# The first expert's first two column blocks: for all tokens, or for gathered tokens like the rest

## The chip, the cores and the metric

The kernel runs on one core of a Trainium2 chip. The metric is the device time of one execution in microseconds (us); lower is better. All times inside the program are counted from the first instruction of the profiled execution.

## The reference

A decoder trunk of two layers on 256 tokens of width 1024 (float32). The first layer ends in a dense channel mixer; the second ends in a mixture of eight experts, and that is the part this change touches:

```python
def swiglu(x, w_gu, w_down):
    gu = jnp.einsum('bsd,df->bsf', x, w_gu)
    g, u = gu[..., :D_FF], gu[..., D_FF:]
    return jnp.einsum('bsf,fd->bsd', jax.nn.silu(g) * u, w_down)

def moe_swiglu(x, w_router, w_gu, w_down):
    logits = jnp.einsum('bsd,de->bse', x, w_router).astype(jnp.float32)
    top_logits, top_idx = lax.top_k(logits, TOP_K)
    top_gates = jax.nn.softmax(top_logits, axis=-1)
    gates = jnp.sum(jax.nn.one_hot(top_idx, N_EXPERTS, dtype=jnp.float32) * top_gates[..., None], axis=-2)
    out = jnp.zeros_like(x)
    for e in range(N_EXPERTS):
        out = out + gates[..., e:e + 1] * swiglu(x, w_gu[e], w_down[e])
    return out
```

D_FF is 2816 (22 blocks of 128 columns), TOP_K is 2 and N_EXPERTS is 8. One expert's weights are 33 units of 1024 KB: 22 for `w_gu`, 11 for `w_down`.

## The kernel before

All weights come through one `Stream` (class at L67). Its list of pieces has a fixed order, a piece is at most 1024 KB, and a piece is loaded as soon as the program knows a free slot for it; in the expert stage there are 17 such slots. The loads are issued by SyncE (SP) in program order, and each waits until TensorE is done with the piece that held the slot. `st.whole()` takes the next piece, `st.passed()` gives its slot back and issues the next load.

An expert's 22 column blocks are cut into chunks, `CH`. A step (e, c) is one chunk of one expert: `up` multiplies the gathered rows of the expert (`xg`, 64 of them) with the chunk's columns of `w_gu`, `up_more` does 32 further rows if the expert has more than 64 tokens (a branch, `more_than_half`), and then `down_both` does the rows of `w_down` that belong to the step before. A step of eight blocks has eight up pieces, which are all given back after the step's branch; only in one step, that of `groups`, are they taken in four groups of two, each with a branch of its own. Small jobs (turning the one-hot matrices, loading counts, the gates) wait in the list `tasks`, and `some(n)` does the next n of them.

Between the last layer norm and the first step stands the router (`first_step`): turn the rows (`turn_rows`), the `logits`, `select` the two best, `number` the tokens of each expert, `count` them, `choose` which expert comes last, build the one-hot matrices (`one_hots`, the first task) and gather (`gather`, eight times). Before the change, the first two column blocks of expert 0 need no gather: `first_columns` multiplies all 256 tokens with them while the router runs, `first_hidden` applies the gate function, and `first_gather` picks expert 0's tokens from the result afterwards:

```python
    def first_columns(pt, tb, k0, k1):
        for k in range(k0, k1):
            mm(pt, xf[tb][:, k], pcs[k // 4][:, k % 4], start=(k == 0))
```

The two pieces that `first_columns` takes are given back by the two calls of `st.passed()` in `first_step`. The loop at the end of `experts` then skips step (0, 0). The rest of the order is written out by hand; nothing reorders it.

Of the kernel before, what the change touches and what calls it, by code (L numbers as in the profile page):

```python
# [12 lines left out]
F32 = mybir.dt.float32  # L13
F32R = mybir.dt.float32r
BF16 = mybir.dt.bfloat16
I32 = mybir.dt.int32
AF = mybir.ActivationFunctionType
OP = mybir.AluOpType
AX = mybir.AxisListType

P = 128
D = 1024
KT = 8
S = 256
TB = 2
# [5 lines left out]
NE = 8  # L31
HALF = 64
CAP = 96
# [12 lines left out]
def trunk_kernel(ctx: ExitStack, tc: tile.TileContext, x, mem, positions, w_in_a, conv_a, w_q_b,  # L46
                 w_kv_shared, w_mem_kv, w_o, ln1_g, ln1_b, ln2_g, ln2_b, w_gu_dense, w_down_dense,
                 w_router, w_gu_moe, w_down_moe, out):
    nc = tc.nc
# [8 lines left out]
    def banks(n=2):  # L58
        return [psum.tile([P, 512], F32, name="pa", tag="pa", bufs=4) for _ in range(n)]

    def bank():
        return psum.tile([P, 512], F32, name="pb", tag="pb", bufs=4)

    def mm(o, l, r, start, stop=True):
        nc.tensor.matmul(o, l, r, start=start, stop=stop, skip_group_check=True)  # L65
# [148 lines left out]
    st = Stream()  # L214
# [3 lines left out]
    def rows(w):  # L218
        return w.rearrange("(k p) c -> p k c", p=P)

    def split(hi, lo, src):
        nc.scalar.copy(hi, src)  # L222
        nc.vector.tensor_sub(lo, src, hi)  # L223
# [21 lines left out]
    def last(gen, tasks=(), every=1):  # L245

        tasks, v = list(tasks), None
        for i, v in enumerate(gen):
            if i % every == every - 1 and tasks:
                t = tasks.pop(0)  # L250
                if t:
                    t()
        for t in tasks:
            if t:
                t()
        return v
# [201 lines left out]
    st.add(*cols(w_kv, MIX, 512), *cols(w_kv, MIX + 512, 256), *wo_specs(1))  # L458


    CH = [[(0, 2), (2, 8), (10, 8), (18, 4)]] + [[(0, 8), (8, 8), (16, 6)]] * (NE - 1)
    order = list(range(FIXED))
    STEPS = [(e, c) for e in range(NE) for c in range(len(CH[e]))]

    def expert_matrix(w, e):

        return w[0, e] if e < FIXED else w[0, bass.ds(order[e], 1)].rearrange("o a b -> (o a) b")

    def expert_up(e, c):
        f0, nf = CH[e][c]  # L470
        w, step = nf * P, PC // (2 * nf * P)

        def piece(k):
            return expert_matrix(w_gu_moe, e).rearrange("(k p) (s f) -> p k s f", p=P, s=2)[
                :, k:k + step, :, f0 * P:f0 * P + w]
        return [(lambda k=k: piece(k), (step, 2, w)) for k in range(0, KT, step)]

    def expert_down(e, c):
        f0, nf = CH[e][c]
        return [(lambda j=j: rows(expert_matrix(w_down_moe, e))[:, f0 + j:f0 + j + 2], (2, D))  # L480
                for j in range(0, nf, 2)]
# [73 lines left out]
    v = last(prod_ws(5, 4, xh, xl), [None, None, load_mem])  # L555
# [6 lines left out]
    v = last(prod_ws(2, 4, xh, xl))  # L562
# [3 lines left out]
    def conv_taps(i):  # L566
        nc.vector.tensor_scalar(yT[:, i], zT[:, i, 2:], cw[:, 12 + i:13 + i], None, op0=OP.mult)
        for k in (1, 0):
            nc.vector.scalar_tensor_tensor(yT[:, i], zT[:, i, k:k + S], cw[:, 6 * k + i:6 * k + i + 1],
                                           yT[:, i], op0=OP.mult, op1=OP.add)  # L570
# [3 lines left out]
    v = last(prod_ws(2, 4, xh, xl), turns, every=2)  # L574
# [5 lines left out]
    v = last(prod_ws(1, 2, xh, xl), [lambda: conv_taps(0), None, lambda: conv_taps(1), None, lambda: conv_taps(2)])  # L580
# [28 lines left out]
    def gate_out(v, i0):  # L609
        for h in range(len(v)):  # L610
# [4 lines left out]
    v = last(prod_ws(2, 4, xh, xl), [None, None, None, units[0].transp, None, units[1].transp, units[0].values,  # L615
                                     units[1].values])
    gate_out(v, 0)
    v = last(prod_ws(1, 2, xh, xl))
# [14 lines left out]
    pcs = []  # L633
# [21 lines left out]
    hT = {}  # L655
# [58 lines left out]
    pcs = st.get(TAIL)  # L714
# [69 lines left out]
    def turn_task(store, tb, i0, n, keys):  # L784
        return lambda: turn_heads(store[tb], tb, i0, n, keys)

    kt, qt = {}, {}
    pcs = st.get(3)
    for tb in range(TB):
        pt = banks()  # L790
# [5 lines left out]
    v = last(prod_ws(1, 2, xh, xl), [None, turn_task(kt, 0, 0, 4, True), None, turn_task(kt, 0, 4, 2, True)])  # L796
# [4 lines left out]
    pcs = st.get(3)  # L801
    pt = banks()
# [3 lines left out]
    pt = banks()  # L806
# [4 lines left out]
    pcs = st.get(3)  # L811
# [14 lines left out]
    pcs = st.get(1)  # L826
# [33 lines left out]
    xf = {}  # L860
# [20 lines left out]
    moe = ctx.enter_context(pool("moe"))  # L881
# [23 lines left out]
    def row_parts(tb):  # L905
        nc.scalar.copy(xth[:, tb], x3[:, tb])
        nc.vector.tensor_sub(xtl[:, tb], x3[:, tb], xth[:, tb])
# [16 lines left out]
        nc.vector.scalar_tensor_tensor(slot, sel, -OFF, ps[:, :2 * NE].rearrange("p (t e) -> p t e", t=TB),  # L924
                                       op0=OP.mult, op1=OP.add)

    pcs = [st.whole() for _ in range(2)]
    hd = {}

    def first_columns(pt, tb, k0, k1):  # L930

        for k in range(k0, k1):
            mm(pt, xf[tb][:, k], pcs[k // 4][:, k % 4], start=(k == 0))

    def first_hidden(tb, pt):
        h = moe.tile([P, 512], F32, name="h", tag="h", bufs=2)
        nc.scalar.activation(h[:, :256], pt[:, :256], AF.Silu)
        nc.vector.tensor_tensor(h[:, :256], h[:, :256], pt[:, 256:], op=OP.mult)
        hd[tb] = moe.tile([P, 2, 256], F32R, name="hd", tag="hx", bufs=2)
        split(hd[tb][:, 0], hd[tb][:, 1], h[:, :256])  # L940

    def router_gates():
        nc.vector.tensor_reduce(mx, lg, axis=AX.X, op=OP.max)
        nc.vector.tensor_tensor(pe, lg, mx[:, :, None].to_broadcast(T3), op=OP.subtract)
# [52 lines left out]
    def experts(part):  # L997
        xg, oneh, turned, hs, hxs, hts, htxs, ys = {}, {}, {}, {}, {}, {}, {}, {}
        tasks = []
# [38 lines left out]
        def groups(e, c):  # L1038

            n = len(expert_up(e, c))  # L1040
            return [2] * (n // 2) if part == 0 and (e, c) == STEPS[1] else [n]

        def up(e, c, n):

            w = CH[e][c][1] * 64
            if up.k == 0:
# [21 lines left out]
        def up_more(e, c, pcs, k):  # L1068
            w = CH[e][c][1] * 64
            g, px = xg[e], up_more.to  # L1070
# [11 lines left out]
        def turn(e, c):  # L1082
            n = CH[e][c][1] // 2
            h = hs.pop((e, c))
# [55 lines left out]
        def scatter_tasks(e):  # L1140
            return [lambda tb=tb, h=h: scatter(e, tb, h) for h in range(2) for tb in range(TB)]

        def first_gather():

            ps = bank()
            for i in range(2):
                for tb in range(TB):
                    for j in range(2):
                        mm(ps[:, i * CAP:(i + 1) * CAP], hd[tb][:, j, i * P:(i + 1) * P], oneh[0][:, tb],
                           start=(i == tb == j == 0))  # L1150
            hts[0, 0] = moe.tile([P, 8, HALF], F32, name="hT", tag="hT", bufs=2)
            htxs[0, 0] = moe.tile([P, 8, CAP - HALF], F32, name="hTx", tag="hTx", bufs=2)
            v = ps[:, :2 * CAP].rearrange("p (a b) -> p a b", a=2)
            nc.scalar.copy(hts[0, 0][:, :2], v[:, :, :HALF])
            nc.vector.tensor_copy(htxs[0, 0][:, :2], v[:, :, HALF:])

        def first_step(gathers):
            pt = banks(2)
            first_columns(pt[0], 0, 0, KT)
            logits(0)  # L1160
            turn_rows(1)
            row_parts(0)
            first_hidden(0, pt[0])
            logits(1)
            select()
            row_parts(1)
            first_columns(pt[1], 1, 0, 6)
            number()
            count()
            first_columns(pt[1], 1, 6, KT)  # L1170
            for _ in range(2):
                st.passed()
            gathers[0]()
            choose()
            for t in gathers[1:1 + KT]:
                t()
            load_orders()
            first_hidden(1, pt[1])
            load_count(0)

        def first_acc():
# [35 lines left out]
        t = batch_tasks(BATCHES[0])  # L1217
        prev = STEPS[0]
        if part == 0:
            first_step(t)  # L1220
            tasks += [first_gather] + t[1 + KT:] + [first_acc]
        else:
            for f in t:
                f()
        for i, (e, c) in enumerate(STEPS):
            if (e, c) == (NE - 1, 2):
                st.retire(raw3)
            for b in BATCHES[1:]:
                if e == b[0] - 1 and c == 0:
                    tasks += batch_tasks(b)  # L1230
            if part == 0 and i == 0:
                continue
            (up_more.to,) = banks(1)
            for g, n in enumerate(groups(e, c)):
                k = up.k
                pcs = up(e, c, n)
                if g == 0:
                    some(3)
                    hxs[e, c] = moe.tile([P, 512], F32, name="hx", tag="hx", bufs=2)
                if g == 0 and i > 0:  # L1240
                    turn_both(prev, prev[0] == e, lambda: up_more(e, c, pcs, k))
                else:
                    with more_than_half(e):
                        up_more(e, c, pcs, k)
                for _ in pcs:
                    st.passed()
            if i > 0:
                down_both(prev, prev[0] == e)
                if prev[1] == len(CH[prev[0]]) - 1:
                    rows_split(prev[0])  # L1250
                    tasks += scatter_tasks(prev[0])
            prev = e, c
# [48 lines left out]
```

## Time and profile before

| what | value |
|---|---|
| median of 3 runs | 1150.37 us (1148.99 to 1150.81) |
| the profiled execution, its own time | 1151.92 us |
| its span, first to last instruction | 1150.2 us |
| TensorE (PE) busy | 1079.8 us, 94% of the span |
| VectorE (DVE) busy | 374.0 us, 33% |
| ScalarE (ACT) busy | 255.4 us, 22% |
| moved by the transfers | 353.79 MB, 308 GB/s over the span |

The profiled execution lies 1.55 us above the median of the three runs. A busy TensorE includes matmuls that run slowly, so its 94% is not a measure of how close it is to its peak. The granted clock of a stretch is 1.00 at 2.4 GHz and 0.50 at 1.2 GHz.

### The profile page before, as it was taken

What the parts mean: (1) busy time and instruction counts of PE and PEld (TensorE: products, weight loads), DVE (VectorE), ACT (ScalarE), POOL (GpSimd) and SP (SyncE); (2) the same over time, 40 slices, a digit from 0 to 9 for tenths busy, and PEclk for the clock granted to TensorE, in tenths of its full rate; (3) what the DMA queues carried; (4) which work ended last, traced back from release to release, by engine and by line L of the source; (5) the groups of instructions that cost most, each with busy time, mean ns of one, the idle gap of its engine ahead of it and who ended that gap; (6) DMA issues with size and microseconds to landing.
All of it is one profiled execution on the core that took longest, in us unless ns stands there. A gap on an engine that the chain in (4) does not pass through costs nothing. (4 is left out here: it accounts for less than half of the span.)

```text
span 1150.2 us, 17136 instructions
## 1 busy us (share of the span) xinstructions
PE 1079.8 (94%) x6958; PEld 640.7 (56%) x6958; DVE 374.0 (33%) x616; ACT 255.4 (22%) x379; POOL 31.7 (3%) x46
## 2 busy tenths in 40 slices
PE   8999999999999899999979998999998999999992
PEld 7988999999887676343323443343333343333330
DVE  5678655454766647010001101100200101200205
ACT  5453544443246522010000000100100100100100
POOL 1000000000100000000000000000000000000002
PEclk9999999999999999998999999899999999999996
DMA  9646565556353369889999999899999999999991
GB/s 332 218 152 215 181 222 199 184 168 216 114 183 126 130 230 361 319 335 408 404 408 409 404 408 409 324 378 402 392 405 409 406 406 409 401 372 404 405 405 51
DMA packets 127590, 353.79 MB, mean 308 GB/s; under 512 B 6375, under 2 KB 41968, under 8 KB 127488
## 3 DMA queue, kind: packets, MB, share of 16 engines
q1 hardware_dynamic: 127392, 352.35, 80.5%
q8 instruction: 69, 1.13, 0.4%
q14 instruction: 33, 0.27, 0.1%
q0 software_dynamic: 96, 0.04, 0.0%
HBM read 351.32 MB, written 1.05 MB: 306 GB/s over the span
## 5 line engine op out<-in xcount | busy, mean ns | idle before, releaser
L65 PE MATMUL pa<-raw,xg 128*64 128x512 f32 (+4 forms) x2304 | 384.6, 555 | 9.3 <-DMA raw<-in_w_gu_moe_dram 8.9
L65 PEld LDWEIGHTS pa<-raw,xg 128*64 128x64 f32 (+1 forms) x2304 | 136.1, 128 | 245.6 <-issue 216.2
L65 PE MATMUL pb<-raw,hT 128*64 128x512 f32 x704 | 161.7, 611 | 6.9 <-ACTq L1196 2.9
L139 DVE TENSOR_TENSOR lo<-raw,hi 128x2048 fp32r<-128x2048 f32 (+2 forms) x68 | 148.5, 2194 | 48.9 <-ACT hi L129 48.8
L65 PE MATMUL pa<-xh,hi 128*128 128x256 f32 x528 | 150.7, 285 | 0.2 <-ACT xh L222 0.2
L129 ACT CAST hi<-raw 128x2048 fp32r<-128x2048 f32 (+2 forms) x68 | 124.5, 1835 | 117.4 <-PE pa L65 73.7
L65 PE MATMUL pa<-xl,hi 128*128 128x256 f32 x528 | 149.6, 283 | 0.3 <-DVE xl L223 0.3
L65 PE MATMUL pa<-xh,lo 128*128 128x256 f32 x528 | 149.3, 283 | 0.0
L1062 DVE TENSOR_TENSOR h<-h,pa 128x512 f32<-128x512 f32 (+2 forms) x24 | 15.3, 638 | 397.6 <-PE pa L65 386.2
L65 PEld LDWEIGHTS pb<-raw,hT 128*64 128x64 f32 x704 | 50.6, 140 | 104.5 <-issue 93.2
L1061 ACT ACTIVATE h<-pa 128x512 f32<-128x512 f32 (+2 forms) x24 | 13.4, 557 | 406.3 <-PE pa L65 406.3
L65 PEld LDWEIGHTS pa<-xh,hi 128*128 128x128 f32 x528 | 101.1, 191 | 1.6 <-issue 0.8
L65 PEld LDWEIGHTS pa<-xl,hi 128*128 128x128 f32 x528 | 101.1, 192 | 0.9 <-DVE xl L223 0.5
L65 PEld LDWEIGHTS pa<-xh,lo 128*128 128x128 f32 x528 | 101.1, 191 | 0.0
L65 PE MATMUL pb<-raw,hTx 128*32 128x256 f32 x704 | 40.3, 380 | 3.9 <-DVE hTx L1098 3.9
L223 DVE TENSOR_TENSOR yl<-pb,yh 64x512 fp32r<-64x512 f32 (+1 forms) x32 | 17.8, 555 | 71.9 <-ACT yh L222 71.9
L65 PE MATMUL pa<-hi,xh 128*128 128x512 f32 (+1 forms) x96 | 35.5, 370 | 0.2 <-ACT xh L222 0.2
L65 PEld LDWEIGHTS pb<-raw,hTx 128*32 128x32 f32 x704 | 22.5, 110 | 21.4 <-DVE hTx L1098 4.4
L1080 DVE TENSOR_TENSOR hx<-hx,pa 64x512 f32<-64x512 f32 (+1 forms) x12 | 7.8, 647 | 80.6 <-ACT hx L1079 65.2
L65 PE MATMUL pa<-lo,xh 128*128 128x512 f32 (+1 forms) x96 | 33.2, 345 | 0.0
L65 PE MATMUL pa<-hi,xl 128*128 128x512 f32 (+1 forms) x96 | 32.7, 345 | 0.0
L222 ACT CAST yh<-pb 64x512 fp32r<-64x512 f32 (+1 forms) x32 | 15.1, 472 | 67.5 <-PE pb L65 54.9
(236 smaller groups left out, 979.6 us busy)
## 6 DMA issues: line engine op xcount, KB each, us to landing
raw<-in_w_gu_moe_dram SPq DMA_DIRECT2D x128, 1024.0 KB, 17.9
raw<-in_w_down_moe_dram SPq DMA_DIRECT2D x88, 1024.0 KB, 16.8
raw<-in_w_gu_moe_dram SPq DMA_DIRECT2D x56, 768.0 KB, 15.9
raw<-in_w_gu_dense_dram SPq DMA_DIRECT2D x44, 512.0 KB, 5.1
raw<-in_w_down_dense_dram SPq DMA_DIRECT2D x11, 1024.0 KB, 4.9
raw<-in_w_in_a_dram SPq DMA_DIRECT2D x8, 1024.0 KB, 9.3
raw<-in_w_o_dram SPq DMA_DIRECT2D x8, 1024.0 KB, 5.0
raw<-in_w_kv_shared_dram SPq DMA_DIRECT2D x6, 1024.0 KB, 5.2
```

Source lines behind the costliest of these rows:

```text
L65: nc.tensor.matmul(o, l, r, start=start, stop=stop, skip_group_check=True)
L129: nc.scalar.copy(hi[:, :n], raw[:, :n])
L139: nc.vector.tensor_sub(v, raw[:, :n].rearrange("p (a b) -> p a b", a=hi.shape[1]), hi)
L222: nc.scalar.copy(hi, src)
L223: nc.vector.tensor_sub(lo, src, hi)
L1061: nc.scalar.activation(h[:, :w], pg[:, :w], AF.Silu)
L1062: nc.vector.tensor_tensor(h[:, :w], h[:, :w], pu[:, :w], op=OP.mult)
L1080: nc.vector.tensor_tensor(h[64:, :w], h[64:, :w], px[64:, :w], op=OP.mult)
```

## The change

Expert 0 gets the same three chunks as the others. `first_columns`, `first_hidden` and `first_gather` go, and with them the two early `st.passed()`; the loop does step (0, 0) like any other, and it is now this step that is taken in four groups of two pieces.

```diff
-    CH = [[(0, 2), (2, 8), (10, 8), (18, 4)]] + [[(0, 8), (8, 8), (16, 6)]] * (NE - 1)
+    CH = [[(0, 8), (8, 8), (16, 6)]] * NE
...
-    pcs = [st.whole() for _ in range(2)]
-    hd = {}
-
-    def first_columns(pt, tb, k0, k1):
...
-    def first_hidden(tb, pt):
-        h = moe.tile([P, 512], F32, name="h", tag="h", bufs=2)
-        nc.scalar.activation(h[:, :256], pt[:, :256], AF.Silu)
-        nc.vector.tensor_tensor(h[:, :256], h[:, :256], pt[:, 256:], op=OP.mult)
-        hd[tb] = moe.tile([P, 2, 256], F32R, name="hd", tag="hx", bufs=2)
-        split(hd[tb][:, 0], hd[tb][:, 1], h[:, :256])
...
-            return [2] * (n // 2) if part == 0 and (e, c) == STEPS[1] else [n]
+            return [2] * (n // 2) if part == 0 and (e, c) == STEPS[0] else [n]
...
-        def first_gather():
...
         def first_step(gathers):
-            pt = banks(2)
-            first_columns(pt[0], 0, 0, KT)
             logits(0)
             turn_rows(1)
             row_parts(0)
-            first_hidden(0, pt[0])
             logits(1)
             select()
             row_parts(1)
-            first_columns(pt[1], 1, 0, 6)
             number()
             count()
-            first_columns(pt[1], 1, 6, KT)
-            for _ in range(2):
-                st.passed()
             gathers[0]()
             choose()
             for t in gathers[1:1 + KT]:
                 t()
             load_orders()
-            first_hidden(1, pt[1])
             load_count(0)
...
-            tasks += [first_gather] + t[1 + KT:] + [first_acc]
+            tasks += t[1 + KT:] + [first_acc]
...
-            if part == 0 and i == 0:
-                continue
```

TensorE's program from the first turned rows to the counts, as a difference (`xf` are the turned rows, `raw` weights, `wr` the router's weights, `r_sel` the selection):

```order
 L867 MATMUL pb<-identf,xt 128x128 x8
-L65 MATMUL pa<-raw,xf 128x512 x8
 L65 MATMUL pb<-wr,xf 128x8 x8
 L867 MATMUL pb<-identf,xt 128x128 x8
 L65 MATMUL pb<-wr,xf 128x8 x8
-L65 MATMUL pa<-raw,xf 128x512 x6
 L65 MATMUL pb<-r_sel,before 128x8
 L65 MATMUL pb<-r_sel,ones 128x8
 L65 MATMUL pb<-r_sel,before 128x8
 L65 MATMUL pb<-r_sel,ones 128x8 x2
-L65 MATMUL pa<-raw,xf 128x512 x2
```

The sixteen wide products of the turned rows are gone; only the small router products are left between the turns and the gather.

SyncE's program before, from the last attention weights to the loading of the experts' order (L989):

```order
L116 DMA raw<-in_w_o_dram 128x2x1024 x4
L114 DMA raw<-in_w_gu_moe_dram 128x4x256 x4
L110 DMA raw<-in_w_gu_moe_dram 128x2x1024 x8
L116 DMA raw<-in_w_down_moe_dram 128x2x1024
L110 DMA raw<-in_w_gu_moe_dram 128x2x1024 x8
L989 TENSOR_LOAD r_cnti
```

The same place with the change:

```order
L116 DMA raw<-in_w_o_dram 128x2x1024 x4
L110 DMA raw<-in_w_gu_moe_dram 128x2x1024 x16
L116 DMA raw<-in_w_down_moe_dram 128x2x1024
L974 TENSOR_LOAD r_cnti
L974 ISA x2
```

Before, a piece of `first_columns` is loaded by two issues of 512 KB, so there are 2 + 8 + 1 + 8 = 19 pieces ahead of the order: 17 for the free slots and 2 for those that the first columns give back. With the change there are 17.

What SyncE issues behind that before, up to the end of the step in groups:

```order
L1196 UNCONDITIONAL_BRANCH x2
L116 DMA raw<-in_w_down_moe_dram 128x2x1024 x2
L1243 COMPARE_AND_BRANCH
L1243 UNCONDITIONAL_BRANCH x2
L116 DMA raw<-in_w_down_moe_dram 128x2x1024 x2
L1243 COMPARE_AND_BRANCH
L1243 UNCONDITIONAL_BRANCH x2
L114 DMA raw<-in_w_gu_moe_dram 128x2x512 x4
L1243 COMPARE_AND_BRANCH
L1243 UNCONDITIONAL_BRANCH x2
L114 DMA raw<-in_w_gu_moe_dram 128x2x512 x4
```

The same with the change:

```order
L1204 UNCONDITIONAL_BRANCH x2
L116 DMA raw<-in_w_down_moe_dram 128x2x1024 x2
L1204 COMPARE_AND_BRANCH
L1204 UNCONDITIONAL_BRANCH x2
L116 DMA raw<-in_w_down_moe_dram 128x2x1024
L110 DMA raw<-in_w_gu_moe_dram 128x2x768
L1204 COMPARE_AND_BRANCH
L1204 UNCONDITIONAL_BRANCH x2
L110 DMA raw<-in_w_gu_moe_dram 128x2x768 x2
L1204 COMPARE_AND_BRANCH
L1204 UNCONDITIONAL_BRANCH x2
L110 DMA raw<-in_w_gu_moe_dram 128x2x768 x2
```

Each group's end lets two slots be filled. Before they take eight full pieces (a piece of 128x2x512 has two issues of 512 KB); with the change three full ones and five of 768 KB, those of the chunk of six blocks.

## Rows read from the trace of the kernel before

**Rows 1.** Windows: us, busy PE, PEld, DVE, ACT, POOL, then clock, transfers' share, GB/s.

```profile
456.14:466.48 10.34, 10.22 (x64) 6.47 (x63) 4.99 (x24) 2.51 (x9) 1.83 (x2) 1.00 0.48 168
...
491.20:498.00 6.80, 5.53 (x28) 2.08 (x26) 2.68 (x14) 3.85 (x5) 0.00 (x0) 1.00 0.29 92
498.00:740.00 242.00, 223.12 (x1349) 87.40 (x1347) 24.75 (x49) 18.45 (x38) 3.68 (x4) 0.97 1.03 407
740.00:750.00 10.00, 10.00 (x74) 4.30 (x74) 1.47 (x3) 1.82 (x4) 0.00 (x0) 1.00 0.30 102
```

**Rows 2.** Timeline of TensorE in expert 2's and expert 5's first step: start, us, instruction, wait.

```profile
594.20 1.94 PE L65 MATMUL pa<-raw,xg 128*64 128x512 f32 x8 [0.62 <-DMA raw<-in_w_gu_moe_dram]
...
872.75 1.94 PE L65 MATMUL pa<-raw,xg 128*64 128x512 f32 x8 [0.62 <-DMA raw<-in_w_gu_moe_dram]
```

**Rows 3.** Timeline of SyncE: when it issued the transfers behind the seventeenth.

```profile
453.22 5.09 SPq L110 DMA_DIRECT2D raw<-in_w_gu_moe_dram  x2
...
466.48 4.69 SPq L116 DMA_DIRECT2D raw<-in_w_down_moe_dram  x4
474.09 6.69 SPq L114 DMA_DIRECT2D raw<-in_w_gu_moe_dram  x8
481.74 14.96 SPq L116 DMA_DIRECT2D raw<-in_w_down_moe_dram  x4
```

**Rows 4.** Issue to landing from dry: L116 at 495.30 (1024 KB), L110 at 747.26 (768 KB).

```profile
DMA to landing us min/median/max: 6.2/6.2/6.2
...
DMA to landing us min/median/max: 4.8/4.8/4.8
```

**Rows 5.** Timeline of TensorE from the turned rows to the first `up`.

```profile
444.71 1.07 PE L867 MATMUL pb<-identf,xt 128*128 128x128 f32 x8
...
448.07 6.83 PE L65 MATMUL pa<-raw,xf 128*128 128x512 f32 x12
454.75 0.28 PE L65 MATMUL pb<-r_sel,before 128*128 128x8 f32 x2
...
457.18 0.77 PE L65 MATMUL pb<-so,xth 128*128 128x192 f32 x2
...
461.22 1.08 PE L65 MATMUL pa<-raw,xg 128*64 128x512 f32 x4
```

**Rows 6.** Timeline of VectorE from the layer norm's end to the one-hot matrices.

```profile
443.12 0.75 DVE L342 SCALAR_TENSOR_TENSOR xt<-xt,rs_z,ln_gb 128x512 f32<-128x512 f32 x1
445.82 0.69 DVE L869 COPY xf<-pb 128x512 f32<-128x512 f32 x1 [1.95 <-PE pb L867]
...
449.88 0.16 DVE L876 COPY lg<-pb 128x8 f32<-128x8 f32 x1
...
451.66 1.22 DVE L907 TENSOR_TENSOR xtl<-xt,xth 128x1024 fp32r<-128x1024 f32 x1
...
456.04 0.80 DVE L1006 TENSOR_SCALAR so<-iota,r_table 128x96 fp32r<-128x96 f32 x4
```

**Rows 7.** Windows around two stretches of half clock, columns as in rows 1.

```profile
447.60:450.90 3.30, 3.30 (x8) 1.75 (x8) 2.28 (x7) 2.35 (x4) 0.00 (x0) 0.50 1.05 425
...
536.30:543.10 6.80, 6.42 (x20) 3.20 (x22) 0.36 (x1) 0.60 (x2) 0.00 (x0) 0.50 1.03 406
```

**Rows 8.** Timeline of TensorE at half clock: two pairs of a gather's matmuls, then `down`.

```profile
537.19 0.63 PE L65 MATMUL pb<-so,xtl 128*128 128x192 f32 x2
...
538.05 0.63 PE L65 MATMUL pb<-so,xtl 128*128 128x192 f32 x2
538.61 5.03 PE L65 MATMUL pb<-raw,hT 128*64 128x512 f32 x12
```

**Rows 9.** Timeline of TensorE: `first_gather`, step (0, 0)'s `down`, step (0, 2)'s `up`.

```profile
464.81 1.10 PE L65 MATMUL pb<-so,hd 128*128 128x96 f32 x8
...
478.92 1.94 PE L65 MATMUL pb<-raw,hT 128*64 128x512 f32 x8 [1.15 <-DVEq L1243]
480.66 13.93 PE L65 MATMUL pa<-raw,xg 128*64 128x512 f32 x64
```

More of the change, by code (lines that the diff above doesn't have):

```diff
@@ L925, in number @@
                                        op0=OP.mult, op1=OP.add)
-    pcs = [st.whole() for _ in range(2)]
-    hd = {}
-    def first_columns(pt, tb, k0, k1):
-        for k in range(k0, k1):
-            mm(pt, xf[tb][:, k], pcs[k // 4][:, k % 4], start=(k == 0))
-    def first_hidden(tb, pt):
-        h = moe.tile([P, 512], F32, name="h", tag="h", bufs=2)
-        nc.scalar.activation(h[:, :256], pt[:, :256], AF.Silu)
-        nc.vector.tensor_tensor(h[:, :256], h[:, :256], pt[:, 256:], op=OP.mult)
-        hd[tb] = moe.tile([P, 2, 256], F32R, name="hd", tag="hx", bufs=2)
-        split(hd[tb][:, 0], hd[tb][:, 1], h[:, :256])
     def router_gates():
@@ L1141, in scatter_tasks @@
             return [lambda tb=tb, h=h: scatter(e, tb, h) for h in range(2) for tb in range(TB)]
-        def first_gather():
[L1145 to L1155, printed above, removed]
         def first_step(gathers):
-            pt = banks(2)
-            first_columns(pt[0], 0, 0, KT)
             logits(0)
```

## The prediction

> **What bounds the kernel now.** I read the windows first. From 498 to 740 us the transfers are busy all the time, at 407 GB/s [rows 1]; one unit of 1024 KB (1.049 MB) takes 2.56 us there, one of 768 KB 1.93. Then I asked whether anybody waits for them, since a busy queue alone bounds nothing: in expert 2's first step, and again in expert 5's, TensorE waits for a weight transfer before each piece [rows 2], one piece per 2.56 us (1.94 of work and 0.62 of waiting). So where experts 2 and 5 begin, time is set by how many bytes have landed by then, and a TensorE that was early or late before has been levelled out. Between those places TensorE may be the later one, and once the transfers wait for it (740 to 750, share 0.30 [rows 1]), but both stretches start from the same state whether or not the whole is shifted. I take it that a shift of the landings before 590 us goes through to the end, one for one.
>
> What can still shift them lies before 498. There the transfers run dry twice: share 0.48 from 456.14 to 466.48 and 0.29 from 491.20 to 498 [rows 1]. In both, all 17 slots are full or held, and SyncE waits until TensorE gives slots back. The timeline of SyncE shows when it could go on: two issues from 453.22 (slots of the first columns), then as the groups of two end (466.48, and 474.09 two groups later, so 3.8 us for each), and nothing between 481.74 and 495.30, while a step of eight pieces is held whole [rows 3]. The question is when the change gives slots back.
>
> **The change part by part.** Count landed units of 1024 KB of expert weights. Before: 17 in the first slots, two from the first columns, four `down` units, four units as eight issues of 512 KB, one more `down` unit: 28. The 29th was issued at 495.30 and needed 6.2 us [rows 4]: 501.5.
>
> *When the first `up` starts.* TensorE began it at 461.22, behind a gather that began at 457.18 [rows 5]. With the change the sixteen wide products are gone. Of these, the last 12 before `number` (448.07 to 454.9 [rows 5]) made it wait: the selection was ready at about 451.7, when VectorE went on to the next job at 451.66 [rows 6]. VectorE also loses two jobs of `first_hidden` that stood ahead of the logits' copy at 449.88 [rows 6].
> The chain is then: layer norm's last half done at 443.87; four turns, half of the 1.07 us of [rows 5]; copy 0.69; rest of row 0's split 1.22, which covers the logits; logits' copy and selection from 449.88 to 451.74, 1.86; split 1.22; slots and counts 0.4; one-hots 0.80 [rows 6]. Together with the semaphore hops (0.1 each) the gather starts at 451.0, and at full clock takes the 4.0 us from 457.18 to 461.22 [rows 5]: `up` starts at 455.0, 6.2 us earlier. Costs at nothing: the table load for the gate function, which moves behind the gather, lies beside 14 us of `up`; the loads of the experts' order on SyncE come right behind the choice and end before the first slot comes free.
>
> *At which clock.* At 447.60 the granted clock was 0.50 for a stretch, after TensorE had done little but turns and logits, and from 536.30 to 543.10 again after a short wait [rows 7]. With the change TensorE has only such small work from the first turned rows to the gather. I take half clock for all of it. Then the turns cost 0.5 more, the logits' second half about 0.9 more that nothing covers any longer, number and count about 1.1 more, and the gather starts at about 453.1. A gather matmul pair is 0.43 us apart at half clock [rows 8] where eight gathers of four took 4.0 us at full; 0.86 per gather. In those stretches matmuls one behind another still ran at half clock for 2.9 us (448.07 [rows 5] to 451.0) and 4.5 us (538.61 [rows 8] to 543.1). With 3 to 5 us of that the gather takes 5.0 to 6.2 us and `up` starts between 458.1 and 459.3. I take 458.8, 2.4 earlier than before.
> The Trainium skill, "TensorE: Matmul & The Clock Gate", section "Part 1: The HAM clock gate", says that the throttled state is the default and that activity releases it. By that rule the wide products removed here were also what kept the clock up; the result would be the one at half clock, and without it the one at full clock below. The two stretches of half clock in this trace agree.
>
> *When slots come back.* The first group ended 5.26 us after its start (466.48 less 461.22); without `first_gather` (464.81 to 465.74 [rows 9]) 4.3. The others follow in 3.8 [rows 3]. So slots come in pairs at 463.1, 466.9, 470.7 and 474.5. Filled in order of the list: three `down` units, then five pieces of 768 KB, because step (0, 2) now has six blocks. The first lands 6.2 us after its issue, the others behind it: 469.3, 471.9, 474.4, then 476.3, 478.3, 480.2, 482.1, 484.1. These eight slots carry 6.75 units; before, the ten slots from 453.22 to 477.9 carried ten.
> Then step (0, 1) holds eight slots whole. It starts at 474.5 with no `down` ahead of it, and gives them back as step (0, 2) did before, 14.6 us after its start (495.30 less 480.66 [rows 9]) plus one load of a count, at most half of the 1.15 us at 478.92 [rows 9]: 489.6. The queue is dry from 484.1 on. The next piece lands 4.8 us after its issue [rows 4], at 494.4, two more by 498.3, then three `down` units: the 29th unit (17 + 3 + 6 + 3) at 505.9.
> From there I see no third dry place: 489.6 gives 7.25 units (18.6 us), `down` of step (0, 0) four more within 9 us, and step (0, 2) eight more at about 510.
>
> *Sum.* 505.9 against 501.5: the landings are 4.4 us later, although `up` starts 2.4 earlier. What is lost is the early return of two slots, and what the later ones carry. The removed 14 us of wide products and the 3.5 us (a quarter of 13.93 [rows 9]) that the larger last chunk adds lie beside transfers. Against the profiled execution's own 1151.92 us that gives 1156.3; that execution lies 1.55 above the median of 1150.37, so 1154.8.
>
> **Rivals.**
> *The clock stays up.* `up` starts at 455.0; everything shifts by 3.8, and the loss is 0.6: 1151.0. For it: the granted clock from 498 to 740 is 0.97 on the mean [rows 1], so half clock is rare. Against: both stretches of [rows 7] followed less idle time than the change leaves here. Chance 0.17.
> *The end follows TensorE, not the transfers.* Then only the start counts: at full clock 6.2 earlier, `first_gather` (0.9) and one `down` step's wait (1.15) saved, 3.5 for the larger chunk added: 4.8 us faster, 1145.6; at half clock 1.0 faster, 1149.4. It decides if TensorE no longer waits for pieces in expert 2's first step, that is if more than some 5 us of slack was in the queue there. Against it stand the waits of [rows 2]. Chance 0.09.
> *The half clock reaches into the first group.* If it lasts until 463, the first group's 3.65 us take up to twice as long: 3.4 more, 1158.2. For it: the stretch of 6.8 us [rows 7]. Chance 0.10.
>
> **How the numbers follow.** The forecast (a shift of 2.5 to 7 us) has 0.62, the remaining 0.02 go to no change at all. A difference of 0.2%, 2.3 us, is about what a measurement of this kernel can tell from none; the clock-stays case lies within it. So slower 0.72 (forecast and the longer half clock), same 0.19, faster 0.09. The range reaches from the clock-stays case, with 0.4 for scatter, 1150.6, to the longer half clock with the same, 1158.6; the faster case lies outside. Most of the chance is on one side, so no second range is needed.
>
> **What would show it.** In the changed profile: a granted clock of 0.50 somewhere between 440 and 460; the first matmul of `xg` between 458 and 460; no issue by SyncE between 446 and 462; five pieces of 768 KB landing by about 484, then a dry stretch until 490 and on; afterwards a share near 1.0 until some 5 us past 740; waits of 0.62 for each piece still there at about 600 and 876. Wrong would be: first `up` at 455 (clock), a dry stretch shorter than 3 us at 487 (release), or the same waits at the same time as before at 594 (the shift was absorbed).

## The result and the profile after

| | before | after |
|---|---|---|
| median of 5 runs each | 1150.37 us (1148.99 to 1152.34) | 1157.08 us (1155.73 to 1159.23) |
| ratio, 95% interval | | 1.0061 [1.0048, 1.0074] |
| profiled execution, its span | 1150.2 us | 1156.4 us |
| TensorE busy in it | 1079.8 us | 1076.9 us |

The changed kernel is 6.7 us slower; the forecast was 4.4. TensorE is busy for 2.9 us less, slow matmuls counted in, and the whole still takes longer.

Windows of the changed kernel, with the columns of [rows 1]: the stretch of half clock, the two dry places, the long busy stretch and the next dry place.

```profile
438.80:459.30 20.50, 15.29 (x68) 14.60 (x69) 13.36 (x48) 3.60 (x7) 0.62 (x2) 0.50 0.76 303
456.00:466.00 10.00, 9.85 (x51) 6.22 (x52) 1.44 (x5) 2.72 (x6) 1.83 (x2) 0.84 0.09 8
485.50:493.00 7.50, 6.23 (x32) 2.46 (x30) 2.31 (x11) 3.50 (x5) 0.00 (x0) 1.00 0.13 20
498.00:740.00 242.00, 217.05 (x1312) 81.32 (x1310) 23.71 (x47) 18.64 (x38) 3.68 (x4) 0.99 1.03 407
747.00:755.00 8.00, 8.00 (x68) 3.70 (x68) 1.47 (x3) 1.82 (x4) 0.00 (x0) 1.00 0.32 101
```

Three things are to be seen. The clock is at its lower level for 20.5 us. In the two dry places, the second of which now comes earlier, the transfers had a share of 0.48 and 0.29 before [rows 1]; now it is 0.09 and 0.13. From 498 to 740 they run at 407 GB/s as before, so nothing is made good there; the later dry place comes some 6 us behind that of [rows 1].

The timeline of TensorE in the changed kernel, against [rows 5, 8, 9]:

```profile
453.61 0.86 PE L65 MATMUL pb<-so,xth 128*128 128x192 f32 x2 [0.71 <-DVE so L991]
...
458.10 0.63 PE L65 MATMUL pb<-so,xth 128*128 128x192 f32 x2
458.53 0.63 PE L65 MATMUL pb<-so,xtl 128*128 128x192 f32 x2
458.96 0.56 PE L65 MATMUL pb<-so,xth 128*128 128x192 f32 x2
459.35 0.38 PE L65 MATMUL pb<-so,xtl 128*128 128x192 f32 x2
...
460.11 3.65 PE L65 MATMUL pa<-raw,xg 128*64 128x512 f32 x16
...
464.49 3.65 PE L65 MATMUL pa<-raw,xg 128*64 128x512 f32 x16
...
476.05 13.95 PE L65 MATMUL pa<-raw,xg 128*64 128x512 f32 x64 [0.15 <-PEq L1204]
489.94 0.66 PE L1073 MATMUL pb<-identf,h 128*128 128x128 f32 x4
```

The gather's pairs follow each other in 0.43 us, as in [rows 8], until 459, so nearly the whole gather runs at half clock; `up` starts at 460.11. Step (0, 1) runs from 476.05 and gives none of its eight slots back before its end.

SyncE in the changed kernel, from five windows of its timeline (issues of one line that follow each other stand in one row, with the waiting between them):

```profile
445.58 23.06 SPq L116 DMA_DIRECT2D raw<-in_w_down_moe_dram  x4
...
464.46 0.89 SPq L116 DMA_DIRECT2D raw<-in_w_down_moe_dram  x2
...
468.26 0.37 SPq L116 DMA_DIRECT2D raw<-in_w_down_moe_dram  x1
...
472.07 1.20 SPq L110 DMA_DIRECT2D raw<-in_w_gu_moe_dram  x2
...
476.02 16.56 SPq L110 DMA_DIRECT2D raw<-in_w_gu_moe_dram  x5
```

The first of the four is the seventeenth piece, at 445.58; the other three are issued at 464.46 (two) and 468.26, behind the first two groups. The third group ends at 472.07 and the fourth at 476.02. Of the five from 476.02, two come at once and three behind step (0, 1), as the next row shows (issues between 489 and 492, and their times to landing):

```profile
L110 SPq DMA_DIRECT2D raw<-in_w_gu_moe_dram x3: 556/559/602, 490.7 to 492.0; - x3
...
DMA to landing us min/median/max: 5.0/7.3/8.7
```

The third `down` unit behind these is the 29th unit; here it stands alone:

```profile
L116 SPq DMA_DIRECT2D raw<-in_w_down_moe_dram x1: 462/462/462, 494.0 to 494.0; - x1
...
DMA to landing us min/median/max: 14.3/14.3/14.3
```

It lands at 494.0 + 14.3 = 508.3; before it landed at 501.5 [rows 4]. That is 6.8 later, and the span is 6.2 longer.

TensorE in expert 2's first step, and in expert 5's, against [rows 2]:

```profile
598.71 1.94 PE L65 MATMUL pa<-raw,xg 128*64 128x512 f32 x8 [0.61 <-DMA raw<-in_w_gu_moe_dram]
601.28 1.94 PE L65 MATMUL pa<-raw,xg 128*64 128x512 f32 x8 [0.64 <-DMA raw<-in_w_gu_moe_dram]
...
868.86 13.90 PE L65 MATMUL pa<-raw,xg 128*64 128x512 f32 x64
```

At the first place it still waits for each piece. At the second it waits no more: all 64 matmuls stand in one row.

### The profile page after: what moved, and what is told of

The parts are those of the page before. It is cut to its first block, busy times and chain, and to the rows that moved or that the text cites. A ratio compares the mean times of both kernels' runs of the same rounds, so it can differ in the third digit from the quotient of the medians.

```text
span 1156.4 us, 17033 instructions
## 1 busy us (share of the span) xinstructions
PE 1076.9 (93%) x6919; PEld 636.9 (55%) x6919; DVE 372.2 (32%) x611; ACT 253.6 (22%) x374; POOL 31.6 (3%) x46
## 5 line engine op out<-in xcount | busy, mean ns | idle before, releaser
L65 PE MATMUL pa<-raw,xg 128*64 128x512 f32 (+3 forms) x2304 | 391.9, 562 | 14.3 <-DMA raw<-in_w_gu_moe_dram 13.5
L1047 DVE TENSOR_TENSOR h<-h,pa 128x512 f32<-128x512 f32 (+1 forms) x24 | 15.4, 643 | 410.3 <-PE pa L65 394.8
L1046 ACT ACTIVATE h<-pa 128x512 f32<-128x512 f32 (+1 forms) x24 | 13.5, 561 | 414.9 <-PE pa L65 414.9
L222 ACT CAST yh<-pb 64x512 fp32r<-64x512 f32 (+1 forms) x32 | 15.1, 471 | 65.2 <-PE pb L65 52.6
```

Source lines behind the costliest of these rows:

```text
L1046: nc.scalar.activation(h[:, :w], pg[:, :w], AF.Silu)
L1047: nc.vector.tensor_tensor(h[:, :w], h[:, :w], pu[:, :w], op=OP.mult)
```

## The experiments

All but the last were timed in five rounds beside the kernel before, whose median was 1150.15 in the first four, 1151.40 in the next four and 1150.53 beside the last two. Two theories stand against each other. **Slots:** what is lost is the number and size of the slots given back ahead of the step that is held whole. **Clock:** what is lost is the half clock in the router. A third, that the end follows TensorE alone, was kept along.

One number of each profile sums up what the transfers lost: the rate from 454 to 500 us, here before and then after:

```profile
454.00:500.00 46.00, 43.13 (x219) 19.63 (x219) 9.88 (x42) 7.30 (x15) 1.83 (x2) 1.00 0.75 280
...
454.00:500.00 46.00, 43.98 (x208) 20.02 (x209) 7.69 (x32) 7.64 (x13) 1.83 (x2) 0.94 0.58 220
```

One GB/s over these 46 us is 0.046 MB, or 0.113 us at 407 GB/s.

| kernel | first `up` | GB/s, 454 to 500 | landings against before, by the rate | span against before | median, ratio to before |
|---|---|---|---|---|---|
| before | 461.22 | 280 | | | 1150.37 |
| after | 460.11 | 220 | +6.8 | +6.2 | 1157.08, 1.0061 [1.0048, 1.0074] |
| 1 after, step (0, 1) in groups too | 459.77 | 285 | -0.6 | -0.3 | 1147.64, 0.9977 [0.9967, 0.9987] |
| 2 after, ten wide products | 457.08 | 259 | +2.4 | +3.7 | 1154.62, 1.0041 [1.0023, 1.0060] |
| 3 before, two slots back behind (0, 1) | 462.87 | 259 | +2.4 | +2.1 | 1152.24, 1.0015 [1.0006, 1.0024] |
| 4 before, two slots back behind (0, 2) | 461.29 | 233 | +5.3 | +6.2 | 1157.02, 1.0056 [1.0043, 1.0068] |
| 5 after, full pieces behind the groups | 460.26 | 256 | +2.7 | +3.8 | 1154.96, 1.0034 [1.0022, 1.0045] |
| 6 before, step (0, 2) in groups too | 461.55 | 324 | -5.0 | -4.6 | 1147.17, 0.9970 [0.9957, 0.9984] |
| 7 as 1, ten wide products | 461.72 | 288 | -0.9 | -3.7 | 1143.15, 0.9948 [0.9928, 0.9968] |
| 8 as 6, and step 1 of experts 1 to 7 | 461.07 | 326 | -5.2 | +0.5 | 1152.65, 1.0016 [1.0006, 1.0026] |
| 9 as 7, wide products spread | 455.85 | 338 | -6.6 | -9.8 | 1142.68, 0.9937 [0.9924, 0.9951] |
| 10 kernel 7 once more, one execution | 455.49 | 340 | -6.8 | -10.2 | 1141.74 |

The two columns of differences agree within 1.5 us, except in 8 and in 7, 9 and 10, where a later dry place shrinks too (242 GB/s from 735 to 755 us before; 290 to 307 in 7, 9 and 10). The landing of the 29th unit itself, taken from the issues and landings of each trace, is nearer still: against before it comes 6.8 us later after the change, and in runs 1 to 6 by -0.7, +3.9, +2.2, +5.6, +3.8 and -4.5. These seven agree with the spans within 0.7 us.

**1. The second step in groups too.**

```diff
-            return [2] * (n // 2) if part == 0 and (e, c) == STEPS[0] else [n]
+            return [2] * (n // 2) if part == 0 and (e, c) in STEPS[:2] else [n]
```

> The changed kernel, with step (0, 1) taken in four groups of two pieces as well. Slot theory (what counts is how much weight the slots given back ahead of the next step that is held whole can carry): step (0, 1) gives its first pair back at about 480.5 instead of all eight at 490.7, so the dry stretch from 485 to 493 goes, the 29th unit lands at about 499 instead of 508.3, and the time falls by about 9 us, to 1148, below the kernel before. Clock theory (the loss is the half clock ahead of the first up): no change, 1157. TensorE theory (the end follows TensorE's work): three branches more, 1157 to 1160.

9.4 us faster than after, 0.2% faster than before, as the slots' theory has it. The profile is of the slowest of its twelve executions (1151.69 us; the fastest took 1145.17). Its windows over the half clock and over the whole place:

```profile
439.60:463.40 23.80, 18.54 (x76) 15.30 (x78) 12.39 (x41) 3.75 (x7) 1.97 (x3) 0.50 0.58 231
454.00:500.00 46.00, 44.09 (x194) 19.33 (x195) 6.86 (x26) 7.67 (x13) 1.83 (x2) 0.90 0.73 285
```

The half clock lasts even longer here, into the first group, and still the loss is gone: with step (0, 1) no longer held whole the second dry place doesn't exist. That speaks against the clock as the main cause.

**2. Wide products put back.** Ten products of the turned rows, of the removed ones' shape, are computed and not used: six ahead of the logits, one, two and one behind the turns, the selection and the counts.

```diff
+            wide(6)
             logits(0)
             turn_rows(1)
+            wide(1)
...
             row_parts(1)
+            wide(2)
             number()
             count()
+            wide(1)
```

> The changed kernel, with ten wide products of turned rows by a weight piece put back into TensorE's waits of the router (6 ahead of the first logits, 1 ahead of the second, 2 ahead of the numbering, 1 ahead of the gather); their results are not used and no slot is given back for them. All theories: the clock is up for more of the router, and the first up starts at about 456 to 457 instead of 460.1. Slot theory: the time falls by just that shift, 3 to 4 us, to 1153 to 1154, and both dry stretches remain. Clock theory: the whole loss comes back, 1150 to 1151.

Windows of the router and of the second dry place, then the first `up`:

```profile
440.00:460.00 20.00, 19.32 (x112) 12.82 (x112) 13.89 (x49) 3.92 (x8) 1.97 (x3) 1.00 0.80 314
...
480.00:490.00 10.00, 8.72 (x44) 3.46 (x42) 2.22 (x11) 3.38 (x5) 0.00 (x0) 1.00 0.15 37
```

```profile
457.08 3.65 PE L65 MATMUL pa<-raw,xg 128*64 128x512 f32 x16
```

At full clock `up` starts 3.0 us earlier, the 29th unit lands 2.9 earlier (505.4) and the median falls by 2.5. The intervals of the two ratios overlap, so the times alone hardly show this gain; the landings of the two profiles do. The second dry place is still there, at a share of 0.15. So the clock is worth about what it moves the start, and most of the loss remains with the clock restored. Two of the nine times stood at 1160.0 and 1160.8, with a mean granted clock of 0.975 and 0.972 over the span against 0.981 to 0.984 in the other seven; no profile of those two was taken.

**3 and 4. The kernel before, with the two slots of the first columns given back later.** The pieces are held, and given back behind step (0, 1), or behind step (0, 2).

```diff
             for _ in range(2):
-                st.passed()
+                held.append(st.raw.pop(st.n_done))
+                st.n_done += 1
...
+                if part == 0 and i == 1 and g == len(groups(e, c)) - 1:
+                    give_back()
```

In run 4 the condition is `i == 2`.

> The kernel before, but the two slots of the first columns are given back only at the end of step (0, 1), at about 478 (two products of 8 columns read them there), still ahead of step (0, 2), which is held whole. Slot theory: the transfers lose two units in the first dry stretch, but the second dry stretch (491 to 498) has room for both; the 29th unit lands at the same time, change 0 to +1 us, 1150 to 1151. Early-return theory (what the change lost is that two slots came back early): the two units are 5 us late, 1155.

> The same, but the two slots are given back only with step (0, 2)'s, at about 495.3. Slot theory: two units fewer can be carried ahead of the step that is held whole, so the 29th unit lands two units later, +5 us, 1155 to 1156. Early-return theory: the same as with the return at 478, 1155. TensorE theory: no change, 1150.

Run 3 is 2.1 us slower than before, a little more than the slots' theory expected. In its profile `up` starts 1.65 later than in [rows 5]. There the clock was at half from 447.4 to 454.2, ahead of the counts, and before only from 447.6 to 450.9 [rows 7]:

```profile
447.40:454.20 6.80, 6.80 (x12) 3.26 (x12) 4.31 (x11) 2.50 (x4) 0.00 (x0) 0.50 1.00 403
```

Taking the later start off one for one, the late return itself costs about half a microsecond, an estimate from this one profile, and no second dry place appears. Run 4 is 6.9 slower, 1 us more than expected. The windows of 3 and then 4:

```profile
454.00:500.00 46.00, 43.30 (x216) 20.22 (x216) 8.65 (x41) 7.30 (x15) 1.83 (x2) 1.00 0.69 259
480.00:500.00 20.00, 17.90 (x86) 7.23 (x87) 2.84 (x15) 3.85 (x5) 0.00 (x0) 1.00 1.03 390
```

```profile
454.00:500.00 46.00, 42.99 (x219) 20.18 (x219) 9.86 (x42) 7.30 (x15) 1.83 (x2) 1.00 0.62 233
480.00:500.00 20.00, 18.58 (x92) 7.73 (x89) 3.84 (x15) 3.85 (x5) 0.00 (x0) 1.00 0.81 295
```

Two slots that come back 22 to 27 us later (from 479.95, and not at 453.2 and 457.8), but still ahead of the step that is held whole, cost next to nothing. Behind it they cost the two units that they would have carried, 2 x 2.56 = 5.1 us and somewhat more.

**5. Full pieces for the eight slots.** Expert 0's last six blocks are taken as a chunk of four and one of two, so that behind the three `down` units come four full pieces.

```diff
-    CH = [[(0, 8), (8, 8), (16, 6)]] * NE
+    CH = [[(0, 8), (8, 8), (16, 4), (20, 2)]] + [[(0, 8), (8, 8), (16, 6)]] * (NE - 1)
```

> The changed kernel, with the last chunk of expert 0 cut into one of four and one of two blocks, so that the five pieces that the last slots ahead of step (0, 1) carry are 1024 KB instead of 768 KB. Slot theory: 1.25 units more are on the way ahead of the dry stretch at 490, the 29th unit lands at about 504.6 instead of 508.3, and the time falls by 3 to 4 us, to 1153 or 1154. Clock theory and TensorE theory: no gain, one step more, 1157 to 1159.

2.1 us faster than after by the medians, 2.4 by the spans, and 3.1 by the two ratios to before, which was 1 us slower beside this run than beside the changed kernel. The rate rises from 220 to 256 GB/s, and the 29th unit lands at 505.3 (expected 504.6). The size of what the slots carry counts as the forecast said.

```profile
454.00:500.00 46.00, 43.82 (x210) 20.01 (x212) 8.21 (x36) 7.65 (x13) 1.83 (x2) 0.95 0.67 256
```

**6. The kernel before, with the step behind the grouped one in groups too.** The condition becomes `(e, c) in STEPS[1:3]`.

> The kernel before, with step (0, 2) taken in groups of two pieces as well. Slot theory: the dry stretch from 491 to 498 goes, the 29th unit lands at about 496 instead of 501.5, and the time falls by about 5 us, to 1145. TensorE theory: three branches more, 1150 to 1152.

4.2 us faster than before (expected 5). The second dry place of [rows 1] is gone:

```profile
480.00:500.00 20.00, 18.63 (x86) 6.86 (x84) 3.60 (x14) 2.68 (x4) 0.00 (x0) 1.00 1.04 398
```

**7 and 10. Runs 1 and 2 together.** Both edits in the changed kernel; 10 is the same kernel once more, for a second profile.

> The changed kernel, with both earlier edits: step (0, 1) in groups, and the ten unused wide products in the router. Slot theory: the two gains add, since one shortens the first dry stretch and the other removes the second: 2.5 us less than with the groups alone, 1145. If the clock were the cause of the whole loss, the groups would add nothing to the wide products, 1154.

> The kernel with both steps in groups and the ten wide products in their first places, once more for a second profile. If the half clock in the router makes the two levels, a time near 1142.5 comes with a full clock from 440 to 460 and a first up at about 457, a time near 1150 with a half clock there and a first up at 460 or later; by the rival the first up doesn't tell the level.

By its median it beats both kernels. Its twelve times stood at two levels: seven from 1141.92 to 1143.19, with a mean granted clock of 0.982 to 0.986 over the span, and five from 1148.34 to 1151.46, with 0.973 to 0.979. The two profiles show one of each level. Window and first `up` of 7 (1148.34 us), then of 10 (1141.74 us):

```profile
445.10:458.70 13.60, 13.60 (x43) 9.47 (x41) 7.45 (x28) 1.84 (x3) 0.00 (x0) 0.50 0.71 278
...
461.72 3.65 PE L65 MATMUL pa<-raw,xg 128*64 128x512 f32 x16
```

```profile
445.10:458.70 13.60, 13.31 (x81) 8.64 (x80) 8.43 (x33) 2.34 (x6) 1.55 (x2) 1.00 0.66 261
...
455.49 3.65 PE L65 MATMUL pa<-raw,xg 128*64 128x512 f32 x16
```

With the same program the clock was at half in the one and full in the other; `up` starts 6.2 us apart, and the spans are 6.5 apart (1146.5 and 1140.0).

**8. More steps in groups.** As 6, and the second step of each expert from 1 to 7.

```diff
-            return [2] * (n // 2) if part == 0 and (e, c) == STEPS[1] else [n]
+            return [2] * (n // 2) if part == 0 and ((e, c) in STEPS[1:3] or (e and c == 1)) else [n]
```

> The kernel before, with step (0, 2) and the second step of each expert from 1 to 7 in groups of two pieces. Slot theory: the dry stretches at 740 and 1005 shrink as well (6.9 and 2.3 us lie there), 1138 to 1142. TensorE theory: 24 branches more in stretches where TensorE is the later one, up to 1 us each, 1150 to 1170.

This expectation was wrong by 10 us or more. Two windows of it:

```profile
735.00:755.00 20.00, 20.00 (x166) 7.03 (x164) 1.74 (x3) 1.55 (x3) 0.00 (x0) 1.00 1.00 374
768.00:777.00 9.00, 8.98 (x88) 4.05 (x88) 0.98 (x2) 1.45 (x3) 0.00 (x0) 1.00 0.34 117
```

The dry place at 740 is filled (before, the first window shows 242 GB/s: 2.6 MB less), but a new one stands at 768 (before: 411 GB/s there, 2.6 MB more). What the groups gave in one step was lost in the next, which is still held whole. The same is seen once more later: the dry place at 1005 (181 GB/s to 1010 before, 404 here) gave way to one at 1033, where before the rate was 408:

```profile
1033.00:1038.00 5.00, 5.00 (x58) 2.24 (x58) 0.98 (x2) 1.08 (x2) 0.00 (x0) 1.00 0.28 71
```

So the last weights land at 1119.7, and in run 6 at 1116.9. Of the 5.1 us between the two spans that is 2.8; the other 2.3 lie behind the last landing (31.0 us against 28.7), and why was not followed up.

**9. The wide products spread.** As 7, with two of the first six moved behind the logits' first half.

```diff
-            wide(6)
+            wide(4)
             logits(0)
+            wide(2)
             turn_rows(1)
```

> The changed kernel with its first two steps in groups and ten unused wide products as in the run before, but two of the first six moved behind the logits' first half, so that no stretch of the router holds small products alone. The twelve times of the run before stood at two levels, 1141.9 to 1143.2 (granted clock 0.982 and up) and 1148.3 to 1151.5 (0.973 to 0.979). If the half clock in the router makes the upper level (first up at 461.7 there, about 457 without it, shifted on one for one now that no step holds the slots), nearly all times here stand at 1142 to 1144. If the two levels come from something later in the program, they come back here in like shares.

All five times lie between 1142.24 and 1144.15, none at the upper level. If seven of twelve were the true share, five low ones in a row would still come up about once in fifteen (7/12 to the fifth power is 0.07), and the two runs were on different chips (4 and 0). So that the spread products remove the upper level is likely, but not shown. Its windows:

```profile
445.10:458.70 13.60, 13.31 (x80) 8.82 (x80) 8.79 (x33) 2.75 (x6) 1.19 (x2) 1.00 0.69 273
454.00:500.00 46.00, 43.60 (x210) 18.10 (x211) 5.89 (x21) 7.13 (x11) 1.84 (x2) 1.00 0.86 338
```

The clock is full and the rate the highest but one of the table. At 0.9937 [0.9924, 0.9951] this is the lowest ratio of the kernels timed in rounds, though its interval overlaps that of run 7: 7.9 us under before, 14.4 under after.

## Why the prediction was right, and where it was off

**What bounds the kernel** held in the sum: the 29th unit lands 6.8 us later and the span is 6.2 longer. But the shift did not go through one for one. By the landings of both traces it is 7.1 us at the 115th of the 264 units, 4.6 at the 132nd, 4.7 at the 215th, 7.1 at the 222nd and 7.3 at the last; the stretch behind the last landing is 1.1 shorter. So it shrinks by 2.6 us around the dry place near 750 and grows by 2.4 around that near 1010. That these two nearly cancel is luck; nothing in the forecast says that they should. At expert 5's first step TensorE no longer waits for pieces, against what the forecast named as a sign. There TensorE was itself late: its first matmul for this step comes 7.9 us later (868.86 against 860.98), and the granted clock was 0.50 from 841.6 to 845.0, where before it was 1.00.

**The clock.** The half clock was forecast, and for the reason given: the wide products gone, only small ones left. It began earlier (438.8) and lasted longer than assumed: 5.7 us of the gather (453.61 to 459.29) rather than 3 to 5. The gather started at 453.6 (forecast 453.1) and `up` at 460.1 (458.8). So `up` came 1.1 us earlier than before and not 2.4: this is the first mis-sized term, 1.3 us. Of it 0.8 is the gather's own length, 6.5 us and not 5.7. The other 0.5 is mostly a slip: the forecast's parts, 451.0 and 0.5, 0.9 and 1.1, add up to 453.5. (No row shows its 0.1 for a semaphore hop, and its "last 12" wide products are six, which the trace lists as twelve records.) The rule of the Trainium skill that was named there ("TensorE: Matmul & The Clock Gate", section "Part 1: The HAM clock gate") is that the throttled state is the default. The changed kernel's 0.50 over 20.5 us agrees. Runs 2, 9 and 10, with wide products, show 1.00 in the router, and run 7 shows 0.50 in spite of them.

**The slots.** First group 4.35 us (forecast 4.3), the next ones 3.8, 3.8 and 4.0 (3.8), step (0, 1) from its start to the return of its slots 14.7 (14.6 and up to half of 1.15, taken as 15.1), next landing 5.0 behind the issue (4.8). From the last landing ahead of the dry stretch to the first behind it went 485.4 to 495.7 (forecast 484.1 to 494.4). These terms held to 0.4, apart from the later start.

**One piece.** The three pieces of 768 KB issued behind step (0, 1) landed at 495.7, 498.7 and 500.7. The second came 3.0 us behind the first, and not 1.93; that is the second mis-sized term, 1.1 us. With 1.3 less 0.2 from the steps between, 0.2 for the landing and 1.1 for this piece the 29th unit is 2.4 later than the 505.9 of the forecast. No stall made the piece late, since the transfers were busy from 493.5 on:

```profile
493.50:498.70 5.20, 5.20 (x26) 1.72 (x24) 1.08 (x2) 0.00 (x0) 0.00 (x0) 1.00 1.03 409
```

How the pieces shared the queue while they came no run here tells.

**The sentence that failed** is "What is lost is the early return of two slots". Run 3 took the early return away and lost about half a microsecond beyond its own later start; run 4 took the two slots out of the stretch ahead of the end of the held step, and lost 6.9. What counts is how much all slots together can carry that come back before a step is held whole: eleven slots with eleven units before, eight with 6.75 now. The difference is 4.25 x 2.56 = 10.9 us; the held step ends 4.6 us earlier (490.7 against 495.3 [rows 3]), which leaves 6.3 of the 6.8. The second half of the sentence, "and what the later ones carry", was shown by run 5.

**The rivals.** "The end follows TensorE" would have made it faster; it was refuted by the result and by runs 3 and 4, in which TensorE has the same work and which lie 4.8 us apart. "The clock stays up" did not happen; run 2 is this case, but for the time of its wide products, and it was still 0.4% slower than before: the forecast's price for it, 0.6 us, was too low, since run 2 loses 4.5 us with `up` at 457.1, and at 455.0, taking 2.1 off one for one, the estimate is 2.4. "The half clock reaches into the first group" happened in run 1 (the group took 5.46 us there), but not in the changed kernel's profile.

## What to carry to other kernels

When a stream of weights is bound by its transfers and one step holds many buffers whole, count how much the buffers can carry that come back ahead of its end; here it mattered little when they came back, as long as it was before the hold (run 3). Giving buffers back in small groups can move the dry place to the next step that is held whole: in runs 1 and 6 it went away, in run 8 it moved from 740 to 768 us. So look at the step behind as well. A wide product that looks like work to be saved can be what keeps the clock up for the chain behind it, so price a removal at both levels of the clock, and expect either from one execution to the next (runs 7 and 10).

## What the runs showed of the hardware

The same program can meet the router at either level: runs 7 and 10 are one kernel, at 0.50 and 1.00 from 445.1 to 458.7, and 6.5 us apart in span. With two of the ten unused products moved between the small ones, five times out of five stood at the lower level, where seven of twelve had been; five are too few to call that shown. In the changed kernel the clock came back only 5.7 us after the start of the gather, whose matmuls follow each other without a gap, and in run 1 only 10.9 us after it (452.6 to 463.5).
